# Splitting queries and keys of a head pair on 128 partitions at once, and spreading the parts by DMA

## The chip, the core and the metric

The kernel runs on one core of a Trainium2 chip. The metric is the device time of one execution in microseconds (us); several executions are made, and their median is compared.

## The reference

Two trunk layers of a latent diffusion block, on 512 latent tokens (a grid of 8 rows by 64 columns) and 256 context tokens of width 1024. Layer 0 mixes by differential attention, layer 1 by neighbourhood attention; each is followed by a squared-ReLU MLP, and both sublayers are normed, modulated and gated from a conditioning vector. What bears on the change:

```python
def rms_norm(x, g):
    xf = x.astype(jnp.float32)
    y = xf * lax.rsqrt(jnp.mean(xf * xf, axis=-1, keepdims=True) + NORM_EPS)
    return (y * g.astype(jnp.float32)).astype(x.dtype)

def diff_attend(q, k, v, lam):                      # layer 0: 8 heads, each a pair (m) of 64 columns
    s = jnp.einsum('bqhmd,bkhmd->bhmqk', q, k).astype(jnp.float32) * ATTN_SCALE
    p = jax.nn.softmax(s, axis=-1)
    w = (p[:, :, 0] - lam * p[:, :, 1]).astype(v.dtype)
    return jnp.einsum('bhqk,bkhe->bqhe', w, v)

    q_l = apply_axial_rope(proj_q(h_lat), cos, sin) # proj_q, proj_kv: h @ w, then rms_norm with a gain
    k_l, v_l = proj_kv(h_lat)
    k_l = apply_axial_rope(k_l, cos, sin)
    k_c, v_c = proj_kv(h_ctx)
    ...
    # layer 1: 16 heads of 64; q_row against a band of rows (with a bias) and all context keys
        s_loc = jnp.einsum('bqhd,brkhd->bhqrk', q_row, k_band).astype(jnp.float32) * ATTN_SCALE
        ...
        s_ctx = jnp.einsum('bqhd,bkhd->bhqk', q_row, k_c).astype(jnp.float32) * ATTN_SCALE
```

## The kernel before

Every float32 matrix operand is kept as two float32r parts, high and low (their sum is the value), and each product is made in three passes, high·high, high·low and low·high. A split of a block is therefore two operations: ScalarE (ACT) copies it with rounding into the high part, VectorE (DVE) or GpSimd (POOL) subtracts that from the source and writes the low part.

For scores of 64-column heads, both parts are stacked on the 128 partitions, so that one matmul contracts over high and low together. A query tile `q[:, m, :]` holds [high; low] for the pair's first head and [low; high] for its second; `kh[:, m, :]` holds the high part of the keys twice, `kl[:, m, :]` the low part twice. Scores are two matmuls, with `kh` and with `kl`.

The work runs in stages. In the profiled execution: setup and the first head's projections to about 90 us, attention of layer 0 to 440, output projection and norm to 560, the MLP to 1110, a transition to 1180, attention of layer 1 to 1500, its output projection to 1560, the second MLP to the end. In an attention stage two streams are interleaved by letters (`run`, with `ORD_HEAD` and `ORD_GROUP`): `attend0` or `attend1` of one head (layer 0) or group of two heads (layer 1), and the projections `qkv0` or `qkv1` of the next. Tokens go in six tiles of 128. `qkv0` steps through them with `tile_(i)` (projection matmuls at L346 into PSUM tile `A`, norm, values, and for the latent tokens the rotation on POOL) and `turn(t)` for pairs of tiles 0, 2 and 4: four transposes by TensorE into one PSUM bank, 256 columns of queries and 256 of keys with the pair's two heads on the lower and the upper 64 partitions, and then `q_split` and `k_split`. The first takes two ACT and two DVE operations of 64x256, the second four of each (the low parts' second copy is a DVE cast, L385). Layer 1 does the same, with queries for the latent tokens alone and with a gain. The turn of tiles 4 and 5 comes last in a head.

Weights come by `wload`: a DMA on SyncE's (SP's) queue into a raw tile `R` (two of them), ACT's copy (L99) and POOL's subtraction (L100) into a weight tile `W` (five of them). `load_qkv` loads the four slices a to d of a head; each holds two of the eight k-tiles, so that the eighth of a projection's k-tiles needs slice d. The modulation matrix is loaded into `R` tiles too (L113, four loads per head in layer 0), and layer 1 loads six bias rows per group on SP (L514). A framework of tiles inserts the waits; its scheduler fixes each engine's order when the program is built. Each queue runs strictly in that order.

Of the kernel before, what the change touches and what calls it, by code (L numbers as in the profile page):

```python
# [18 lines left out]
P = 128  # L19
# [15 lines left out]
# the order of the interleaved streams, by letters (see run)  # L35
# [5 lines left out]
# the PSUM tiles of each phase  # L41
# [8 lines left out]
class Block:  # L50
# [40 lines left out]
    def wload(self, src, n, tile=None, eng=None):  # L91
        """a weight slice [128, n] as its float32r parts: [:, 0] high, [:, 1] low."""
# [10 lines left out]
    def mod_load(self, l, n, early=False):  # L103
        """256 columns of the modulation matrix, as eight k-tiles."""
# [12 lines left out]
    def setup(self):  # L117
# [13 lines left out]
        # silu(c), silu(c_ctx), padded to 32 columns  # L131
# [8 lines left out]
        # modulation scalars: [layer][norm] -> A (gain*(1+scale)), B (shift)  # L140
# [28 lines left out]
        # lambda  # L169
# [66 lines left out]
    def normed(self, halves):  # L236
        """x rows (two halves of 512) -> x * rstd as one [128, 1024] tile."""
# [13 lines left out]
    def modulated(self, xns, tiles, l, norm, hT, tag):  # L251
        """transposes, modulates and splits the token tiles into hT."""
# [20 lines left out]
    def normed_early(self, xs):  # L273
        """the first norm, transposed, ahead of the modulation: 4 tiles of two k-tiles each."""
# [90 lines left out]
    def q_split(self, ps, q, cols, gain=None):  # L365
        """transposed queries of two heads -> stacked [H;L] (head 0), [L;H] (head 1)."""
        nc = self.nc
        lo, hi = slice(0, 64), slice(64, 128)
        for m, (a, b) in enumerate(((lo, hi), (hi, lo))):
            if gain is None:  # L370
                nc.scalar.activation(q[a, m, cols], ps[a], AF.Copy)
                nc.vector.tensor_sub(q[b, m, cols], ps[a], q[a, m, cols].bitcast(F32))
            else:
                nc.scalar.activation(q[a, m, cols], ps[a], AF.Copy, scale=gain[a])
                nc.vector.scalar_tensor_tensor(q[b, m, cols], ps[a], gain[a], q[a, m, cols].bitcast(F32),
                                               op0=ALU.mult, op1=ALU.subtract)

    def k_split(self, ps, kh, kl, cols):
        nc = self.nc
        lo, hi = slice(0, 64), slice(64, 128)  # L380
        for m, (a, b) in enumerate(((lo, hi), (hi, lo))):
            nc.scalar.activation(kh[a, m, cols], ps[a], AF.Copy)
            nc.vector.tensor_sub(kl[a, m, cols], ps[a], kh[a, m, cols].bitcast(F32))
            nc.scalar.activation(kh[b, m, cols], ps[a], AF.Copy)
            nc.vector.tensor_copy(kl[b, m, cols], kl[a, m, cols].bitcast(F32))  # L385

# [1 line left out]
    def load_qkv(self, w, g):  # L388
        return [self.wload(w[g, s], 768) for s in range(4)]

    def qkv0(self, w, hT, out, accs=None, tag='Q'):
# [26 lines left out]
        def turn(i):  # L418
# [7 lines left out]
            self.q_split(ps[:, 0:256], q, cols)  # L426
            self.k_split(ps[:, 256:512], kh, kl, cols)
# [10 lines left out]
    def attend0(self, h, qkv, last=None):  # L438
# [10 lines left out]
        for i in range(NT):  # L449
# [15 lines left out]
            # w = p0 - lam p1, up to the factor 1/sum0, which the output takes  # L465
# [40 lines left out]
    def bias1(self, g):  # L506
        """rpb of the windows (two heads, three kinds of tile) plus the window's mask, keys reversed."""
# [12 lines left out]
    def qkv1(self, w, hT, out, tag='H'):  # L520
# [16 lines left out]
        def turn(i0):  # L537
            ps = self.pst('A')
            for j in range(2):
# [20 lines left out]
    def attend1(self, g, qkv, last=None):  # L560
# [5 lines left out]
        for jp in range(2):  # L566
            for m in range(2):
# [19 lines left out]
                # the window that straddles tiles: [a 64 | b 128 | c 64] -> blocks b and [c | a]  # L587
# [110 lines left out]
    def mlp(self, l, t0, xh, hT, tag, mid, done, side):  # L698
# [36 lines left out]
        def blend():  # L735
            """x + gate * (the sum so far), beside the last matrix products."""
# [44 lines left out]
class Mods:  # L781
    """the modulation chunks, in order, each loaded well before its products."""
# [28 lines left out]
def hybrid_block(tc, a, out):  # L811
    nc = tc.nc
    with ExitStack() as ctx:
# [6 lines left out]
        with b.psum_phase("ps0", **PS_HEAD0):  # L820
# [4 lines left out]
            w = b.load_qkv(a["wqa"], 1)  # L825
            for _ in b.qkv0(None, hT, cur, accs):
                pass
        with b.psum_phase("psA", **PS_ATTN0):
            att = b.attend0(0, cur)
            run(mods, ORD_FIRST, a=att)  # L830
            for h in range(1, HEADS0):
                nxt = []
                qkv = b.qkv0(w if h == 1 else b.load_qkv(a["wqa"], h), hT, nxt)
# [29 lines left out]
        with b.psum_phase("psC", **PS_ATTN1):  # L863
            cur = []
            run(mods, "Q", q=b.qkv1(w1, hT1, cur))
            for g in range(GROUPS1):
                nxt, last = [], [] if g + 1 == GROUPS1 else None
                att = b.attend1(g, cur, last)
                if last is None:
                    w = b.load_qkv(a["wqb"], g + 1)  # L870
                    run(mods, ORD_GROUP, a=att, q=b.qkv1(w, hT1, nxt))
                else:
                    run(mods, ORD_OUT1, a=att, q=b.project(1, a["wob"], b.oT1, last, 2, lambda i: b.x2[i - 2], 'Q', 'H', 'S1', nxt))
# [16 lines left out]
def lay_out(i):  # L890
# [8 lines left out]
    # rotary tables, in the order of the permuted latents  # L899
# [55 lines left out]
```

## Time and profile before

| what | value |
|---|---|
| median of 3 runs | 1934.52 us (1934.1 to 1935.02) |
| span of the profiled execution | 1928.0 us |
| instructions | 27111 |
| busy: TensorE (PE) / DVE / ACT / POOL | 94% / 63% / 42% / 40% |
| DMA packets and bytes | 58723, 185.02 MB |

The span is that of the instructions of one execution under the profiler. The runs' times contain what lies around it: the median is 6.5 us longer. In rows of the profile, an instruction is given by engine, line, operation and `out<-in` with the names of the tiles (numbers left out); `SPq` and `ACTq` are the parts of an engine's queue that issue DMAs. PE counts matmuls, PEld the loading of weights into TensorE beside them.

### The profile page before, as it was taken

To read this page: it belongs to the slowest core of one execution; us is meant where nothing else is said; L and a number is where in the kernel's file an instruction comes from. 1 tells how busy PE (TensorE), PEld (TensorE's weight loads), DVE (VectorE), ACT (ScalarE), POOL (GpSimd) and SP (SyncE) were. 2 spreads that over 40 slices of the span, in tenths; PEclk is the share of its full clock that TensorE was granted. 3 is DMA by queue.
4 is the path that set the end of the run, shared out by engine and by line. 5 is a ranking of instruction groups with operands and counts; after the bars stand their busy time and mean duration, and the time that the engine had idled before them with its cause. 6 is when DMAs were issued, how large, how long until landed. Compare 5 with 4: busy or idle time off the path is not lost.

```text
span 1928.0 us, 27111 instructions
## 1 busy us (share of the span) xinstructions
PE 1809.4 (94%) x10256; PEld 1574.1 (82%) x10256; DVE 1205.3 (63%) x2349; ACT 812.5 (42%) x1819; POOL 770.6 (40%) x620
## 2 busy tenths in 40 slices
PE   6899999997899999999999988998998989999998
PEld 5788888885688888888888968998897778888886
DVE  4688888887664343343334685988889664444447
ACT  4466666666342221221221244666656342232231
POOL 3655555544222221221222443444543334344443
PEclk9999999998999999999999998999998999999999
DMA  7222222225222332332432241223323223323331
GB/s 296 92 67 71 86 85 74 73 69 195 84 89 90 118 120 91 128 124 95 131 113 74 57 125 41 50 62 74 77 72 99 93 77 100 97 87 94 103 94 71
DMA packets 58723, 185.02 MB, mean 96 GB/s; under 512 B 7328, under 2 KB 13792, under 8 KB 54496
## 3 DMA queue, kind: packets, MB, share of 16 engines
q1 hardware_dynamic: 52848, 173.44, 29.1%
q10 hardware_dynamic: 5744, 9.85, 1.4%
q8 instruction: 80, 1.31, 0.3%
q14 instruction: 51, 0.42, 0.1%
HBM read 174.45 MB, written 8.81 MB: 95 GB/s over the span
## 4 chain that ended last, share of the span: by engine, by line
PE 67%; DVE 15%; DMA 6%; ACT 4%; POOL 4%; issue 4%; SPq 1%; ACTq 0%; POOLq 0%; DVEq 0%
PE PD L719 23%; PE PA L753 11%; PE PB L753 10%; PE PA L346 9%; PE PA L651 4%; PE PA L200 2%; DMA X<-in_rpb_dram 2%; PE PS L458 2%; PE PB L485 1%; POOL W L100 1%; PE PQ L335 1%; DVE SA L581 1%; DMA N<-oT 1%; DMA R<-in_wmod_dram 1%; DVE N L604 1%
## 5 line engine op out<-in xcount | busy, mean ns | idle before, releaser
L100 POOL TENSOR_TENSOR W<-R,W 128x1024 fp32r<-128x1024 f32 (+1 forms) x200 | 451.0, 2262 | 700.8 <-ACT W L99 700.7
L99 ACT ACTIVATE W<-R 128x1024 fp32r<-128x1024 f32 (+1 forms) x204 | 200.9, 994 | 457.8 <-PE PB L753 364.2
L719 PE MATMUL PD<-Q,W 128*128 128x384 f32 (+1 forms) x1584 | 291.4, 332 | 1.1 <-DVE Q L270 0.5
L719 PEld LDWEIGHTS PD<-Q,W 128*128 128x128 f32 x1584 | 269.5, 188 | 16.6 <-issue 7.0
L346 PE MATMUL PA<-W,H 128*128 128x384 f32 x1008 | 201.8, 347 | 5.1 <-DVE T L209 4.4
L728 DVE TENSOR_TENSOR N<-N 128x768 f32<-128x768 f32 (+1 forms) x64 | 61.9, 969 | 220.3 <-ACT N L727 110.7
L346 PE MATMUL PA<-W,Q 128*128 128x384 f32 (+1 forms) x1008 | 186.7, 332 | 10.9 <-DVE H L535 5.6
L719 PE MATMUL PD<-H,W 128*128 128x512 f32 (+1 forms) x816 | 187.6, 386 | 3.4 <-DVE H L271 2.5
L346 PEld LDWEIGHTS PA<-W,H 128*128 128x128 f32 x1008 | 176.3, 191 | 13.0 <-DVE T L209 4.9
L719 PEld LDWEIGHTS PD<-H,W 128*128 128x128 f32 x816 | 148.9, 191 | 36.3 <-DVE H L271 2.7
L346 PEld LDWEIGHTS PA<-W,Q 128*128 128x128 f32 x1008 | 162.7, 198 | 13.3 <-DVE H L535 7.0
L753 PE MATMUL PA<-W,H 128*128 128x512 f32 x648 | 168.1, 399 | 2.7 <-DVE T L759 2.5
L233 POOL TENSOR_TENSOR SQ<-SQ,half 128x4 f32<-128x4 f32 (+1 forms) x96 | 93.9, 979 | 161.0 <-DVE SQ L231 133.9
L753 PEld LDWEIGHTS PA<-W,H 128*128 128x128 f32 x648 | 119.2, 188 | 32.9 <-issue 6.2
L753 PE MATMUL PB<-W,H 128*128 128x512 f32 x504 | 132.3, 394 | 0.0
L753 PE MATMUL PA<-W,Q 128*128 128x512 f32 x432 | 108.7, 391 | 2.2 <-ACT Q L730 1.7
L753 PEld LDWEIGHTS PB<-W,H 128*128 128x128 f32 x504 | 94.5, 188 | 19.4
L764 DVE TENSOR_TENSOR H<-PA,H 128x512 f32<-128x512 f32 x78 | 53.7, 688 | 78.6 <-PE PA L753 78.6
L753 PEld LDWEIGHTS PA<-W,Q 128*128 128x128 f32 x432 | 80.9, 188 | 21.1 <-ACT Q L730 2.4
L464 ACT ACTIVATE E<-PS,SA 128x768 f32<-128x768 f32 (+1 forms) x96 | 72.7, 758 | 34.4 <-DVE SA L463 33.8
L463 DVE TENSOR_REDUCE SA<-PS 128x1 f32<-128x768 f32 (+1 forms) x96 | 74.4, 775 | 20.2 <-ACT E L464 13.6
L753 PE MATMUL PB<-W,Q 128*128 128x512 f32 x336 | 85.3, 389 | 0.0
(213 smaller groups left out, 3177.1 us busy)
## 6 DMA issues: line engine op xcount, KB each, us to landing
R<-in_w_dram SPq DMA_DIRECT2D x128, 512.0 KB
W<-in_wmod_dram SPq DMA_DIRECT2D x32, 1024.0 KB
R<-in_wmod_dram SPq DMA_DIRECT2D x32, 512.0 KB
R<-in_wqa_dram SPq DMA_DIRECT2D x32, 384.0 KB
R<-in_wqb_dram SPq DMA_DIRECT2D x32, 384.0 KB
X<-in_rpb_dram SPq DMA_DIRECT2D x48, 128.0 KB
R<-in_woa_dram SPq DMA_DIRECT2D x8, 512.0 KB
R<-in_wob_dram SPq DMA_DIRECT2D x8, 512.0 KB
```

Source lines behind the costliest of these rows:

```text
L99: nc.scalar.activation(w[:, 0, :n], raw, AF.Copy)
L100: (eng or nc.gpsimd).tensor_sub(w[:, 1, :n], raw, w[:, 0, :n].bitcast(F32))
L200: nc.tensor.matmul(ps[32 * q:32 * q + 32, 0:256], self.silu[:, kt, :], raws[kt], start=kt < 4, stop=kt >= 4)
L233: nc.gpsimd.tensor_tensor(r, ss, self.half[:, :n], op=ALU.pow)
L346: nc.tensor.matmul(acc[:, :n], hT[kt][:, x, P * i:P * i + P], w[kt // 2][:, y, o:o + n], start=(kt == 0 and p == 0), stop=(kt == KT - 1 an ...
L463: nc.vector.tensor_reduce(mx, s, op=ALU.max, axis=AX, negate=True)
L464: nc.scalar.activation(e[:, m, :nk], s, AF.Exp, bias=mx[:, 0:1], accum_out=sm[:, m:m + 1])
L651: nc.tensor.matmul(ps, oHL[h][:, x, c:c + P], w[h // 2][:, y, 512 * (h % 2):512 * (h % 2) + 512], start=(h == hs[0] and p == 0), stop=(h = ...
L719: nc.tensor.matmul(ps[:, at:at + b1 - b0], w[kt // 4][:, x, o:o + P], hT[kt][:, y, b0:b1], start=(kt == 0 and p == 0), stop=(kt == KT - 1 ...
L728: nc.vector.tensor_mul(r, r, r)
L753: nc.tensor.matmul(ps, hd[:, x, P * i - c0:P * i - c0 + P], w[f][:, y, 512 * n:512 * n + 512], start=(f == 0 and p == 0), stop=(f == len(h ...
L764: nc.vector.tensor_add(av, ps, av)
```

## The change

`q_split` and `k_split` are replaced by three functions. `hl_split` splits the whole transposed block of a turn at once, one ACT and one DVE operation on 128 partitions (512 columns in layer 0; in layer 1 256 for the keys and, with the gain, 256 for the queries), into two scratch blocks `h` and `l`. `q_spread` and `k_spread` copy these to the stacked layout by DMAs of 64x256 on SP's queue: 4 for the queries, 8 for the keys. The scratch is the last 512 columns of the weight tiles themselves: `load_qkv` now allocates four tiles of 2048 columns, of which the weights use 1536. Turns 0 and 4 use the tails of the first two tiles, turn 2 those of the other two. The first group of layer 1, whose weights lie elsewhere, allocates four weight tiles for the purpose.

```diff
+    def hl_split(self, ps, h, l, gain=None):
+        nc = self.nc
+        if gain is None:
+            nc.scalar.activation(h, ps, AF.Copy)
+            nc.vector.tensor_sub(l, ps, h.bitcast(F32))
+        else:
+            nc.scalar.activation(h, ps, AF.Copy, scale=gain)
+            nc.vector.scalar_tensor_tensor(l, ps, gain, h.bitcast(F32), op0=ALU.mult, op1=ALU.subtract)
+
+    def q_spread(self, h, l, q, cols):
         nc = self.nc
         lo, hi = slice(0, 64), slice(64, 128)
         for m, (a, b) in enumerate(((lo, hi), (hi, lo))):
...
+            nc.sync.dma_start(q[a, m, cols].bitcast(F32), h[a].bitcast(F32))
+            nc.sync.dma_start(q[b, m, cols].bitcast(F32), l[a].bitcast(F32))
+
+    def k_spread(self, h, l, kh, kl, cols):
         nc = self.nc
         lo, hi = slice(0, 64), slice(64, 128)
...
+        for src, dst in ((h, kh), (l, kl)):
+            for m, a in enumerate((lo, hi)):
+                for b in (lo, hi):
+                    nc.sync.dma_start(dst[b, m, cols].bitcast(F32), src[a].bitcast(F32))
...
     def load_qkv(self, w, g):
-        return [self.wload(w[g, s], 768) for s in range(4)]
+        ts = [self.wpool.tile([P, 2048], F32R, tag="W", name=self._name("W")) for _ in range(4)]
+        return [self.wload(w[g, s], 768, t[:, 0:1536].rearrange("p (a n) -> p a n", a=2))
+                for s, t in enumerate(ts)], ts
+
+    def scratch(self, ts, k):
+        return [t[:, 1536:2048] for t in ts[2 * (k % 2):2 * (k % 2) + 2]]
...
-            self.q_split(ps[:, 0:256], q, cols)
-            self.k_split(ps[:, 256:512], kh, kl, cols)
+            h, l = self.scratch(room, i // 2)
+            self.hl_split(ps, h, l)
+            self.q_spread(h[:, 0:256], l[:, 0:256], q, cols)
+            self.k_spread(h[:, 256:512], l[:, 256:512], kh, kl, cols)
...
+            h, l = self.scratch(room, i0 // 2)
+            self.hl_split(ps[:, 0:256], h[:, 0:256], l[:, 0:256])
+            self.k_spread(h[:, 0:256], l[:, 0:256], kh, kl, slice(P * i0, P * i0 + 256))
             if i0:
-                self.q_split(ps[:, 256:512], q, slice(P * i0 - 256, P * i0), gain=self.gqk)
-            self.k_split(ps[:, :256], kh, kl, slice(P * i0, P * i0 + 256))
+                self.hl_split(ps[:, 256:512], h[:, 256:512], l[:, 256:512], gain=self.gqk[:, 0:1])
+                self.q_spread(h[:, 256:512], l[:, 256:512], q, slice(P * i0 - 256, P * i0))
...
+            room = [b.wpool.tile([P, 2048], F32R, tag="W", name=b._name("W")) for _ in range(4)]
+            run(mods, "Q", q=b.qkv1(w1, room, hT1, cur))
```

The order of the engines moves with it. The rows below are of heads 3 and 4 of layer 0 (each row is line, operation, `out<-in` with the tiles' numbers, shape; "x3" is three alike). On SP before, the loads of a head's four weight slices follow each other between loads of the modulation matrix (`R508`, `R509`, and `R642` behind):

```order
L113 DMA R508_2402<-in_wmod_dram 128x1024
L113 DMA R509_2403<-in_wmod_dram 128x1024
L95 DMA R625_2960<-in_wqa_dram 128x768
L95 DMA R627_2965<-in_wqa_dram 128x768
L95 DMA R629_2970<-in_wqa_dram 128x768
L95 DMA R631_2975<-in_wqa_dram 128x768
L113 DMA R642_3022<-in_wmod_dram 128x1024
```

On SP after, head 3's spreads stand between slice c (`R631`) and slice d (`R632`) of head 4's weights: first turn 0's, then turn 2's (out of `W475`, `W476`), then turn 4's (out of `W473`, `W474`); the rows from turn 2's keys on:

```order
L390 DMA Q482_2314<-W475_2295 64x256 x4
L390 DMA Q483_2315<-W476_2296 64x256 x4
L380 DMA Q481_2313<-W473_2293 64x256 x2
L381 DMA Q481_2313<-W474_2294 64x256 x2
L390 DMA Q482_2314<-W473_2293 64x256 x4
L390 DMA Q483_2315<-W474_2294 64x256 x4
L95 DMA R632_3000<-in_wqa_dram 128x768
```

What moved: slice d's load was behind slice c's, and now is behind 36 DMAs, of which the last 12 need the head's last split. On ACT before, three of the next head's slices (`W628`, `W630`, `W632`, L99) are split ahead of turn 2's queries (`PC585`, L371):

```order
L99 ACTIVATE W628_2967<-R627_2965 128x768
L99 ACTIVATE W630_2972<-R629_2970 128x768
L384 ACTIVATE Q482_2296<-PC541_2575 64x256
L354 ACTIVATE Y602_2861<-PA601_2836 128x256
L401 ACTIVATE Q484_2298<-PA601_2836 128x128
L99 ACTIVATE W632_2977<-R631_2975 128x768
L371 ACTIVATE Q481_2295<-PC585_2777 64x256
```

On ACT after, slice b (`W626`) comes behind turn 2's split (row L369 of `PC585`, ten rows earlier) and ahead of an exponential (L478) and of turn 4's split (`PC624`):

```order
L99 ACTIVATE W626_2985<-R630_2992 128x768
L478 ACTIVATE E607_2900,SA608_2901<-PS609_2902,SA610_2911 128x768
L369 ACTIVATE W473_2293<-PC624_2965 128x512
L502 ACTIVATE O596_2845<-PB595_2840,SA591_2829 128x128
L461 ACTIVATE N564_2715<-PB600_2855,subg_122 128x128
L99 ACTIVATE W627_2986<-R631_2996 128x768
```

What moved: slices b, c and d of the next head now come behind splits of this one, and slice b's tile is one out of which turn 2's spreads read. On PE after, between the last projection of head 3 and the first product of head 4 that needs slice d (`W628`) stand the scores of one query tile of head 2 and two of head 3, with their outputs; the rows at the end:

```order
L499 MATMUL PB617_2935<-Q330_1621,X614_2922 128x256 x12
L460 MATMUL PB622_2958<-ident_69,O555_2664 128x128
L472 MATMUL PS646_3052<-Q483_2315,Q481_2313 128x256
L472 MATMUL PS646_3052<-Q482_2314,Q481_2313 128x256
L472 MATMUL PS646_3052<-Q483_2315,Q481_2313 128x256
L472 MATMUL PS646_3052<-Q482_2314,Q481_2313 128x512
L472 MATMUL PS646_3052<-Q483_2315,Q481_2313 128x512
L460 MATMUL PB623_2961<-ident_69,O620_2952 128x128
L346 MATMUL PA637_3008<-W628_2987,H94_542 128x384
```

What stands there now: the product with slice d is in PE's queue behind the scores of head 3 that read the spread keys (`Q482`, `Q483`), and everything later stands behind it.

More of the change, by code (lines that the diff above doesn't have):

```diff
@@ L369, in q_split, with qkv0 @@
         for m, (a, b) in enumerate(((lo, hi), (hi, lo))):
[L370 to L378, printed above, removed]
+            nc.sync.dma_start(q[a, m, cols].bitcast(F32), h[a].bitcast(F32))
+            nc.sync.dma_start(q[b, m, cols].bitcast(F32), l[a].bitcast(F32))
+    def k_spread(self, h, l, kh, kl, cols):
         nc = self.nc
         lo, hi = slice(0, 64), slice(64, 128)
[L381 to L385, printed above, removed]
-    def load_qkv(self, w, g):
-        return [self.wload(w[g, s], 768) for s in range(4)]
-    def qkv0(self, w, hT, out, accs=None, tag='Q'):
+        for src, dst in ((h, kh), (l, kl)):
+            for m, a in enumerate((lo, hi)):
+                for b in (lo, hi):
+                    nc.sync.dma_start(dst[b, m, cols].bitcast(F32), src[a].bitcast(F32))
+    def load_qkv(self, w, g):
+        ts = [self.wpool.tile([P, 2048], F32R, tag="W", name=self._name("W")) for _ in range(4)]
[3 more added lines that the diff above has]
+        return [t[:, 1536:2048] for t in ts[2 * (k % 2):2 * (k % 2) + 2]]
+    def qkv0(self, w, room, hT, out, accs=None, tag='Q'):
         nc = self.nc
@@ L518, in bias1, with qkv1 @@
         return b
-    def qkv1(self, w, hT, out, tag='H'):
+    def qkv1(self, w, room, hT, out, tag='H'):
         nc = self.nc
@@ L824, in hybrid_block @@
             b.setup_layer0(*tabs)
-            w = b.load_qkv(a["wqa"], 1)
-            for _ in b.qkv0(None, hT, cur, accs):
+            w, room = b.load_qkv(a["wqa"], 1)
+            for _ in b.qkv0(None, room, hT, cur, accs):
                 pass
@@ L832, in hybrid_block @@
                 nxt = []
-                qkv = b.qkv0(w if h == 1 else b.load_qkv(a["wqa"], h), hT, nxt)
+                if h > 1:
+                    w, room = b.load_qkv(a["wqa"], h)
+                qkv = b.qkv0(w, room, hT, nxt)
                 att2 = b.attend0(h, nxt, last if h + 1 == HEADS0 else None)
@@ L869, in hybrid_block @@
                 if last is None:
-                    w = b.load_qkv(a["wqb"], g + 1)
-                    run(mods, ORD_GROUP, a=att, q=b.qkv1(w, hT1, nxt))
+                    w, room = b.load_qkv(a["wqb"], g + 1)
+                    run(mods, ORD_GROUP, a=att, q=b.qkv1(w, room, hT1, nxt))
                 else:
```

2 lines of the change are left out of this document (removed).

## The prediction

> **What bounds the kernel now.** I read the page from the top: the span, the busy time of each engine, then stretches of each attention layer, and last what TensorE (PE) waited for in them.
>
> ```profile
> span 1928.0 us, 27111 instructions
> PE 1809.4 (94%) x10256; PEld 1574.1 (82%) x10256; DVE 1205.3 (63%) x2349; ACT 812.5 (42%) x1819; POOL 770.6 (40%) x620
> 140.00:440.00 300.00, 280.17 (x1864) 252.30 (x1864) 244.70 (x585) 197.87 (x565) 159.37 (x195) 0.99 0.26 82
> 1180.00:1500.00 320.00, 293.49 (x1948) 280.84 (x1947) 274.78 (x650) 198.97 (x506) 138.95 (x143) 0.96 0.25 68
> ```
>
> The last two rows are a table of stretches (start:end, length, then busy PE, PEld, DVE, ACT, POOL, granted clock, DMA share, GB/s): six heads of layer 0, seven groups of layer 1. PE is busy 94% of the span. It idles 300 − 280.2 = 19.8 us in the first stretch (3.3 per head of 50 us) and 320 − 293.5 = 26.5 us in the second (3.8 per group). DVE comes next, at 82% and 86% of these stretches. The PE's waits, first in layer 0 and then in layer 1 (total us, times, longest):
>
> ```profile
> PE PA L200 <- DMA R<-in_wmod_dram: 5.3, 6, 1.5
> PE PB L485 <- DVE X L481: 4.6, 6, 1.8
> PE PC L424 <- ACT Q L384: 0.4, 1, 0.4
> PE PA L346 <- POOL W L100: 0.2, 1, 0.2
> ...
> PE PA L346 <- DVE H L535: 5.6, 4, 2.2
> PE PA L346 <- ACT H L384: 3.1, 1, 3.1
> PE PS L575 <- DVE H L375: 1.5, 1, 1.5
> PE PS L575 <- ACT H L384: 0.6, 1, 0.6
> ```
>
> The splits that the change rewrites make PE wait 0.4 us in six heads of layer 0, and 5.2 us in seven groups of layer 1. The projection (L346) hardly ever waits for its weights in layer 0: 0.2 us.
>
> **What it takes away.** The splits per turn, and the nearest rows for the wide ones that replace them:
>
> ```profile
> L384 ACT ACTIVATE Q<-PC 64x256 fp32r<-64x256 f32 x42 | 15.9, 378 | 9.0 <-DVE Q L383 8.4
> L372 DVE TENSOR_TENSOR Q<-PC,Q 64x256 fp32r<-64x256 f32 x42 | 17.7, 422 | 3.0 <-ACT Q L371 1.7
> L385 DVE CAST Q<-Q 64x256 fp32r<-64x256 f32 x48 | 24.1, 503 | 1.5
> L603 ACT ACTIVATE N<-PB x64: 577/598/605, 1213.0 to 1523.3; 128x512 fp32r<-128x512 f32 x64
> L604 DVE TENSOR_TENSOR N<-PB,N x64: 671/686/693, 1213.9 to 1524.0; 128x512 fp32r<-128x512 f32 x64
> ```
>
> A turn of layer 0 was 6 ACT x 0.38 = 2.3 us and 4 x 0.42 + 2 x 0.50 = 2.7 us on DVE; now it is one of each, 0.60 and 0.69 by the same shape at L603 and L604. That is 1.7 and 2.0 us a turn, over 24 turns 41 and 48 us; layer 1 gives about as much less, some 30 on each. None of it lies on PE's path but through PE's waits. Layer 0 can win between 0 and its 19.8 idle us; I take 1.3 per head, since the probabilities' splits (L481, 4.6) wait on a DVE that gets freer. In layer 1 I take the 5.2 us of the splits, the 5.6 behind L535 (it stands in DVE's queue, beside the splits) and 2 us of clock (below): 13 together, with bounds of 0 and 26.5.
>
> **What it adds: the spreads.** Each turn now issues 12 DMAs of 64x256 (64 KB) on SP's queue, the same queue that loads weights: 36 per head, 32 per group, 544 in all, of which before has none. Three rows bound SP's time for one:
>
> ```profile
> L210 ACTq DMA_DIRECT2D gates<-T x16: 229/237/257, 77.5 to 1036.4; - x16
> L95 SPq DMA_DIRECT2D R<-in_wqa_dram x32: 327/328/1651, 10.9 to 374.9; - x32
> L514 SPq DMA_DIRECT2D X<-in_rpb_dram x48: 537/591/667, 1138.5 to 1428.5; - x48
> 1225.69 1.25 SPq L514 DMA_DIRECT2D X<-in_rpb_dram  x2
> 1223.79 5.45 DMA X<-in_rpb_dram
> ```
>
> A plain block issued from SP is 0.33 us (L95), the nearest in form, so c = 0.33; ends 0.24 (a small transfer, on ACT's queue) and 0.59 (many short runs, L514). The last two rows, of the timeline and of the chain of waits, give the landing: the pair's issue ends at 1226.94, its bytes are there at 1229.24, 2.3 us later. The spreads of a turn thus take 12 x 0.33 + 2.3 = 6.3 us from the first issue to the last landing; ends 5.2 and 9.4. In the changed order each also waits for the one eight issues earlier, which at 2.3 us of landing asks for 0.33 too.
>
> By the Trainium skill (DMA: Bandwidth & Descriptors, Anatomy of one DMA) a transfer costs about 2 us plus its bytes at 436 GB/s, so a turn's 768 KB would be an estimated 3.8 us if the bytes and not the issues set it; the rows above say that issuing does, and no run here shows the other yet.
>
> **Where it meets PE in layer 0.** The parts wait in the last columns of the head's own four weight tiles, so a weight tile comes free for the next head only when the spreads that read it have landed. With five tiles, the next head's slice a is in the fifth, b and c take the tiles of turn 2's scratch, d takes one of turn 4's; d's load also stands on SP behind turn 4's spreads. Turn 0 and turn 4 share scratch too, but turn 0's spreads are a tile's projection older. So the end of a head becomes a chain, which the before kernel spreads under the projection. Its pieces:
>
> ```profile
> 219.00 0.33 SPq L95 DMA_DIRECT2D R<-in_wqa_dram  x1
> 222.14 0.84 ACT L99 ACTIVATE W<-R 128x768 fp32r<-128x768 f32 x1 [2.58 <-DMA R<-in_wqa_dram]
> 223.47 1.81 POOL L100 TENSOR_TENSOR W<-R,W 128x768 fp32r<-128x768 f32 x1
> 201.23 0.90 ACT L464 ACTIVATE E<-PS,SA 128x768 f32<-128x768 f32 x1
> 200.26 0.39 ACT L354 ACTIVATE Y<-PA 128x256 f32<-128x256 f32 x1 [1.61 <-PE PA L346]
> 211.77 0.73 POOL L416 TENSOR_TENSOR Y<-Y,Y 128x256 f32<-128x256 f32 x1
> ```
>
> A slice lands 222.14 − 219.33 = 2.8 us after its issue. With t = 0 at the end of the head's last projection matmul: turn 2's transposes lie 0.9 us before it; their split (0.60 + 0.69, two handovers) has both parts at 0.6. Twelve issues end at 4.6, the last lands at 6.9. Only then ACT splits slice b (0.84, to 7.7), an exponential follows (0.90, to 8.6), and turn 4's split stands behind both: done at 9.9. Turn 4's transposes must be there too: norm and rotation of the last tile took from 200.26 to 212.50 in before, its own pieces are about 5 us; I take 7.5, since nothing long stands ahead of it now; it hides under the 8.6, and at its 12.2 adds 3.6. Twelve issues to 13.9, slice d's issue and landing 0.33 + 2.8 to 17.0, its split on ACT and POOL 0.84 + 1.81 to 19.7.
>
> What PE has in the meantime, in the changed order, up to the first matmul that reads slice d: 19 projection matmuls (L346), 20 of scores (L458 in before), 20 of output (L485), 10 transposes of probabilities (L478) and 11 short ones:
>
> ```profile
> 202.06 4.28 PE L346 MATMUL PA<-W,H 128*128 128x384 f32 x23
> 206.18 0.49 PE L478 MATMUL PB<-ident,E 128*128 128x128 f32 x3
> 207.10 1.66 PE L458 MATMUL PS<-Q,Q 128*128 128x512 f32 x8
> 211.24 1.59 PE L485 MATMUL PB<-Q,X 128*128 128x256 f32 x12
> ```
>
> That is 19 x 0.186 = 3.5; 20 scores at up to 0.207, the narrow ones less, 3.5; 20 x 0.12 of output (they overlap a little) = 2.4; and 21 transposes and short ones at 0.09 to 0.16, some 2.0: 11.4 us, of which I count 11.3. So PE stands still for 19.7 − 11.3 = 8.4 us at each head's end. With c = 0.24 it is 6.2, with 0.59 14.9, with the slow transposes 12. Of the present 3.3 us per head 2 stay, after the 1.3 of relief: 8.4 + 2 − 3.3 = 7.1 us more per head. There are seven ends of a head; the one of head 0, whose projections run apart, I count half: 6.5 x 7.1 = 46 us. Ends: 6.5 x (6.2 − 3.3) = 19, where all present idling goes, and 6.5 x 14.9 = 97, where none does.
>
> **The clock.** After a wait PE is slower for a while:
>
> ```profile
> 1303.56 1.81 PE L346 MATMUL PA<-W,Q 128*128 128x256 f32 x13 [1.26 <-DVE H L535]
> 1311.89 4.85 PE L346 MATMUL PA<-W,Q 128*128 128x256 f32 x21 [3.09 <-ACT H L384]
> ```
>
> The same matmul took 0.139 us after a gap of 1.26 and 0.231 after 3.09: some 2 us lost in the 21. The 8.4 us are cut into pieces by exponentials and transposes, of which I expect one over 3 us in about every fourth head: 3 us; ends 0 and 6.5 x 2 = 13. The Trainium skill (TensorE: Matmul & The Clock Gate, Why this matters for your kernels) wants no idle gap above about 3 us; the two rows agree with it, and by it a single gap of 8.4 us would cost each head the 2 us, 13 in place of my 3.
>
> **Layer 1.** There three slices of a later group and its six bias rows stand on SP ahead of a group's spreads and one behind, the group has 32 spreads in place of 36, and its period of 45 us leaves SP idle for most of it. 32 x 0.33 = 10.6 us of issue fit. I take 0.5 us per group of new waits, 4 us, and 3 us more for the first group, whose scratch takes four weight tiles of its own, while its spreads stand behind twelve bias rows. With the 13 of relief that is −6; ends +15 and −25.
>
> **The sum.** 46 + 3 (clock) − 6 (layer 1) = 43 us on the span of 1928.0: 1971. The runs' median is 1934.5, 6.5 above the span, and I keep that distance: 1934.5 + 43, some 1977.
>
> **The rivals.** First, *the spreads are cheap and hide, and the engines' relief wins*: a 64 KB issue takes 0.1 us. Then turn 2's spreads are landed at 0.6 + 1.2 + 2.3 = 4.1, slice b's split and the exponential end at 5.8, the transposes are there (their own pieces, 5 us), turn 4's split ends at 7.1, its issues at 8.3, slice d is in at 11.4 and split at 14.1: PE waits 2.8 us per head, and if one more stays of the 3.3, layer 0 loses 6.5 x 0.5 = 3. Layer 1 gives its 13 and up to half as much again: 1934.5 + 3 − 17 = 1920. The place is L346's wait for slice d; it decides for faster where that wait is under about 3 us a head. Against it: no issue on SP's queue in these rows is under 0.33, and PE's wait at 0.24 is already twice 3 us.
>
> Second, *both effects cancel*: c at 0.24 (+19 in layer 0) against a layer 1 at −20: 1934.
>
> Third, *a half-height transfer costs what the L514 rows cost*: c = 0.59, wait 14.9 us per head, and layer 1's 19 us of issue per group then push the bias rows (its chain already has 5.45 us of DMA X): 6.5 x (14.9 + 2 − 3.3) = 88, and some 1.5 us a group, 12: 2035. In its favour stands a rule of the Trainium skill (DMA: Bandwidth & Descriptors, Rules for kernel authors): two transfers on the two halves of the partitions share the same engines, so that one of 128 rows does better. What hangs on it is that 12 of half height would cost like 12 of full height; no run here shows that yet.
>
> **How the numbers follow.** About 0.2%, 4 us, is what a measurement of this kernel can tell from no change. Chances: the forecast, 1945 to 2010, 0.63; the first rival 0.18; the second 0.05; the third 0.14. The likeliest is 1977. The range takes in the second rival and most of the first and of the third: 1920 to 2032. Faster 0.18, same 0.05, slower 0.77.
>
> **What would show it.** In the profile after: ACT's and DVE's instructions fall by 208 each (5 a turn in layer 0, 3 or 4 in layer 1), their busy time by some 70 us each; SP shows 544 transfers of L380, L381 and L390 at 0.33 us. In the stretch of layer 0 PE's waits have a new first row, L346 waiting for POOL's or ACT's split of W, with some 50 us where 0.2 stood, and ACT's L99 waits for DMAs out of W. The head period grows from 50 to about 57. In layer 1 L346's waits for L384's successor vanish. I am wrong if L346 has no such wait (issues are cheap, or the transposes come early), or if PE loses as much in layer 1: then SP's queue has no room there either.

## The result, and the profile after

The changed kernel took 2008.03 us (median of 4 runs, 2004.88 to 2012.18), the kernel before 1934.31 us beside it: a ratio of 1.0383, 95% interval 1.0362 to 1.0404, 74 us slower. The two profiles are of single executions, and their spans differ by 82 us and not by 74, since the one before, 1928.0 us, is some 5 us shorter than is usual for that kernel (43 executions beside the runs below have spans of 1927.1 to 1943.8, the middle one 1932.7), and the one after is the longest of its four. The top of its page:

```profile
span 2010.4 us, 27956 instructions
PE 1843.5 (92%) x10256; PEld 1583.8 (79%) x10256; DVE 1102.3 (55%) x2141; ACT 735.0 (37%) x1611; POOL 765.9 (38%) x620
```

The freed engines are there: 208 instructions less on DVE and on ACT, 103 and 78 us of busy time. PE's 10256 matmuls are the same, but their records add up to 34 us more. To see where the span grew, both traces are cut where a stage's first instruction starts: first projection of layer 0 to the first MLP (L719 before, L736 after), that MLP, and first score of layer 1 to the second MLP. The table of stretches, before and then after (start:end, length, busy PE, PEld, DVE, ACT, POOL, clock, DMA share, GB/s):

```profile
66.70:561.00 494.30, 450.13 (x2753) 392.23 (x2754) 386.87 (x898) 300.24 (x836) 239.59 (x273) 0.97 0.27 84
561.00:1110.10 549.10, 548.02 (x3089) 478.04 (x3088) 238.45 (x323) 127.09 (x167) 157.25 (x70) 1.00 0.33 108
1192.10:1555.90 363.80, 333.16 (x2118) 311.10 (x2117) 302.65 (x689) 216.27 (x535) 150.80 (x147) 0.95 0.26 70
```

```profile
68.90:605.70 536.80, 470.48 (x2753) 397.53 (x2754) 337.02 (x778) 260.05 (x716) 238.54 (x273) 0.95 0.38 113
605.70:1154.80 549.10, 547.98 (x3089) 477.95 (x3088) 238.35 (x323) 126.89 (x167) 157.46 (x70) 1.00 0.34 108
1238.90:1637.60 398.70, 341.26 (x2102) 311.40 (x2103) 255.06 (x597) 181.89 (x449) 154.44 (x149) 0.95 0.42 108
```

Layer 0 is 42.5 us longer, 22 of it idle PE and 20 longer records of the same matmuls; layer 1 is 34.9 longer, 27 and 8 (with 16 matmuls fewer between its marks). The MLP is unchanged to 0.1 us.

The longer records have two parts that the traces show. First, the trace grants the clock either in full or at half: at half for 34.1 us of layer 0's stretch before and 51.2 after, and for 34.1 and 42.8 of layer 1's. Half of the difference, 8.5 and 4.4 us, is the most that this can cost. Second, a projection matmul alone has a record of 0.337 us, but 23 in a row take 4.28 us, 0.186 each; so each further break in a row of matmuls adds some 0.15 us to the busy time, without PE doing more (an estimate from these two numbers). PE stops 104 times in layer 0's stretch after and 59 before, 74 and 45 times in layer 1's: 7 and 4 us. The two parts together are 15 of the 20 us and the 8.

What one spread costs SP, by line (duration min/median/max in ns):

```profile
L390 SPq DMA_DIRECT2D Q<-W x192: 461/595/1932, 78.3 to 498.2; - x192
L390 SPq DMA_DIRECT2D H<-W x192: 461/595/2095, 1221.0 to 1562.6; - x192
L95 SPq DMA_DIRECT2D R<-in_wqa_dram x32: 327/328/1452, 11.2 to 438.3; - x32
```

595 ns for a spread, while a weight load of six times the bytes stays at 328. The end of a head, SP, ACT's weight splits and PE in the timeline:

```profile
239.73 1.10 SPq L380 DMA_DIRECT2D Q<-W  x2
240.93 1.18 SPq L381 DMA_DIRECT2D Q<-W  x2
242.16 6.24 SPq L390 DMA_DIRECT2D Q<-W  x8
248.50 1.17 SPq L380 DMA_DIRECT2D Q<-W  x2
249.77 1.18 SPq L381 DMA_DIRECT2D Q<-W  x2
251.00 5.07 SPq L390 DMA_DIRECT2D Q<-W  x8
256.16 0.53 SPq L95 DMA_DIRECT2D R<-in_wqa_dram  x1
...
246.27 0.84 ACT L99 ACTIVATE W<-R 128x768 fp32r<-128x768 f32 x1
250.29 0.84 ACT L99 ACTIVATE W<-R 128x768 fp32r<-128x768 f32 x1 [1.30 <-DMA Q<-W]
259.68 0.84 ACT L99 ACTIVATE W<-R 128x768 fp32r<-128x768 f32 x1 [1.02 <-DMA R<-in_wqa_dram]
...
240.32 0.68 PE L346 MATMUL PA<-W,H 128*128 128x384 f32 x3
260.06 0.30 PE L460 MATMUL PB<-ident,O 128*128 128x128 f32 x1 [1.69 <-DVE O L508]
260.58 0.44 PE L346 MATMUL PA<-W,H 128*128 128x384 f32 x1 [0.22 <-ACT W L99]
262.47 1.97 PE L346 MATMUL PA<-W,H 128*128 128x384 f32 x5 [0.57 <-POOL W L100]
```

From 239.73 to 256.07 SP does nothing but issue 24 spreads, 16.3 us in a row. (In five other heads of this layer they are two rows of 12, 7.5 to 8.2 us each, with 0.6 to 1.5 us between them.) Slice d's load (256.16) stands behind them, lands at 259.68, and PE's first product with it starts at 260.58, 19.6 us after the last projection of the old head (241.0); the next ones, which need POOL's part of slice d too, start at 262.47. PE is busy for 12.5 of the 19.6 us and stands still for 7.1. But this idle time isn't in one place. PE's waits from head to head in layer 0 (us in total, times, longest):

```profile
PE PA L346 <- POOL W L100: 8.3, 14, 1.0
PE PB L460 <- DVE O L508: 8.0, 6, 1.7
PE PS L472 <- ACT E L478: 7.0, 10, 2.8
PE PB L499 <- ACT X L494: 4.8, 10, 0.6
PE PA L346 <- ACT W L99: 4.8, 6, 1.1
PE PS L472 <- DMA Q<-W: 3.4, 7, 1.0
```

The weights' splits (L99, L100) make 13 us in six heads; most of the rest is PE at the short chains of attention, one after the other, where no projection stands between them in its queue. In layer 1 the same row of spreads stands at the end of a group:

```profile
1325.03 4.97 SPq L390 DMA_DIRECT2D H<-W  x8
...
1332.84 5.02 SPq L390 DMA_DIRECT2D H<-W  x8
...
1340.51 1.04 SPq L95 DMA_DIRECT2D R<-in_wqb_dram  x2
1346.60 1.73 ACT L99 ACTIVATE W<-R 128x768 fp32r<-128x768 f32 x2 [3.15 <-DMA R<-in_wqb_dram]
1347.49 1.11 PE L346 MATMUL PA<-W,Q 128*128 128x256 f32 x3 [2.48 <-ACT W L99]
```

24 issues in 15.4 us, to 1340.4; the next weights behind them; PE waits 2.48 us for these, where in layer 1 before L346 waited longest for splits of DVE and ACT (L535, L384). Its waits in seven groups:

```profile
PE PS L592 <- ACT E L599: 10.5, 9, 2.8
PE PB L619 <- DVE T L635: 10.0, 8, 1.6
PE PS L592 <- DMA H<-W: 9.6, 14, 2.1
PE PB L629 <- DVE N L621: 6.3, 10, 1.4
PE PA L346 <- ACT W L99: 5.7, 5, 2.5
PE PA L346 <- POOL W L100: 5.0, 5, 1.1
```

The waits of L346 for DVE's and ACT's H are gone; in their place scores wait for landings (DMA H<-W, 9.6) and for exponentials, and L346 for the weights' splits, 10.7 us.

### The profile page after: what moved, and what is told of

Its sections match the earlier page's. It is cut to its first block, busy times and chain, and to the rows that moved or that the text cites. A ratio compares the mean times of both kernels' runs of the same rounds, so it can differ in the third digit from the quotient of the medians.

```text
span 2010.4 us, 27956 instructions
## 1 busy us (share of the span) xinstructions
PE 1843.5 (92%) x10256; PEld 1583.8 (79%) x10256; DVE 1102.3 (55%) x2141; ACT 735.0 (37%) x1611; POOL 765.9 (38%) x620
## 2 busy tenths in 40 slices
DMA packets 102248, 220.76 MB, mean 110 GB/s; under 512 B 16032, under 2 KB 57312, under 8 KB 98016
## 5 line engine op out<-in xcount | busy, mean ns | idle before, releaser
L100 POOL TENSOR_TENSOR W<-R,W 128x1024 fp32r<-128x1024 f32 (+1 forms) x200 | 451.2, 2265 | 741.1 <-ACT W L99 721.6
L99 ACT ACTIVATE W<-R 128x1024 fp32r<-128x1024 f32 (+1 forms) x204 | 200.4, 993 | 457.7 <-PE PB L770 364.3
L736 PE MATMUL PD<-Q,W 128*128 128x384 f32 (+1 forms) x1584 | 291.3, 332 | 1.1 <-DVE Q L270 0.6
L736 PEld LDWEIGHTS PD<-Q,W 128*128 128x128 f32 x1584 | 269.4, 188 | 16.7 <-issue 7.0
L346 PE MATMUL PA<-W,H 128*128 128x384 f32 x1008 | 210.2, 352 | 16.0 <-POOL W L100 8.9
L346 PEld LDWEIGHTS PA<-W,H 128*128 128x128 f32 x1008 | 176.5, 192 | 31.1 <-POOL W L100 15.5
L346 PE MATMUL PA<-W,Q 128*128 128x384 f32 (+1 forms) x1008 | 186.5, 331 | 12.4 <-POOL W L100 6.0
L736 PE MATMUL PD<-H,W 128*128 128x512 f32 (+1 forms) x816 | 188.3, 387 | 3.3 <-DVE H L271 2.5
L736 PEld LDWEIGHTS PD<-H,W 128*128 128x128 f32 x816 | 149.6, 193 | 36.3 <-DVE H L271 2.7
L346 PEld LDWEIGHTS PA<-W,Q 128*128 128x128 f32 x1008 | 160.8, 195 | 17.6 <-POOL W L100 8.2
L472 PE MATMUL PS<-Q,Q 128*128 128x256 f32 (+1 forms) x320 | 78.5, 370 | 12.4 <-ACT E L478 7.9
L499 PE MATMUL PB<-Q,X 128*128 128x256 f32 x448 | 74.0, 301 | 16.6 <-DVE X L495 11.4
```

Source lines behind the costliest of these rows:

```text
L99: nc.scalar.activation(w[:, 0, :n], raw, AF.Copy)
L100: (eng or nc.gpsimd).tensor_sub(w[:, 1, :n], raw, w[:, 0, :n].bitcast(F32))
L346: nc.tensor.matmul(acc[:, :n], hT[kt][:, x, P * i:P * i + P], w[kt // 2][:, y, o:o + n], start=(kt == 0 and p == 0), stop=(kt == KT - 1 an ...
L472: nc.tensor.matmul(s[:, c0:c1], q[:, m, P * i:P * i + P], k[:, m, c0:c1], start=p == 0, stop=p == 1)
L499: nc.tensor.matmul(po[:, :256], wT[:, x, P * kt:P * kt + P], v[:, kt].rearrange("p a d -> p (a d)"), start=(x, kt) == jobs[0], stop=(x, kt ...
L736: nc.tensor.matmul(ps[:, at:at + b1 - b0], w[kt // 4][:, x, o:o + P], hT[kt][:, y, b0:b1], start=(kt == 0 and p == 0), stop=(kt == KT - 1 ...
```

## The experiments

The theories: (1) SP's time for each issue, some 0.6 us, in rows of 24, holds the next weights and the scores; (2) the scratch holds the weight tiles until the spreads have landed; (3) the added bytes disturb. Beside the times, each profile gives two marks: the start of the first MLP, which carries layer 0, and the time from there to the start of the second, which carries layer 1 (the MLP in it is constant). A mark is read from one execution. Where a layer is as before, it came out 2.7 us later (layer 0 in the kernel with layer 1 alone) and 0.5 us earlier (layer 1 in the kernel with layer 0 alone), so a few us between two marks tell nothing. The two differences of marks add up to 3 to 8 us more than the difference of the times.

| kernel | time, us | before beside it | ratio (95%) | first MLP starts | to the second |
|---|---|---|---|---|---|
| before | 1934.31 | | | 561.0 | 994.9 |
| the change | 2008.03 | 1934.31 | 1.0383 (1.0362 to 1.0404) | 605.7 | 1031.9 |
| layer 0 alone | 1971.82 | 1936.44 | 1.0179 (1.0163 to 1.0194) | 602.1 | 994.4 |
| layer 1 alone | 1970.65 | 1936.44 | 1.0170 (1.0155 to 1.0186) | 563.7 | 1031.2 |
| free spreads | 1915.76 | 1936.44 | 0.9894 (0.9877 to 0.9911) | 566.3 | 972.3 |
| high parts on ACT's queue | 2025.35 | 1936.44 | 1.0453 (1.0428 to 1.0477) | 613.8 | 1042.5 |
| weights on ACT's queue | 1976.19 | 1934.04 | 1.0219 (1.0193 to 1.0245) | 584.9 | 1019.5 |
| own scratch, layer 0 | 1991.97 | 1934.04 | 1.0299 (1.0272 to 1.0325) | 584.9 | 1031.3 |
| own scratch, layer 1 | 2027.47 | 1934.16 | 1.0475 (1.0450 to 1.0501) | 601.8 | 1050.1 |
| six spreads a turn | 1952.09 | 1934.04 | 1.0095 (1.0065 to 1.0125) | 566.0 | 1011.5 |
| six, and weights on ACT | 1947.68 | 1934.16 | 1.0064 (1.0038 to 1.0090) | 568.6 | 1006.0 |
| three spreads a turn | 1944.93 | 1935.33 | 1.0050 (1.0032 to 1.0067) | 562.3 | 1009.0 |
| two for the keys' copies | 1931.78 | 1934.04 | 0.9988 (0.9974 to 1.0002) | 567.9 | 992.5 |
| keys' copies on POOL | 1947.29 | 1934.16 | 1.0061 (1.0041 to 1.0080) | 570.2 | 1002.9 |

**One layer at a time.** The other layer keeps its old splits and its own load of weights:

```diff
-            self.hl_split(ps, h, l)
-            self.q_spread(h[:, 0:256], l[:, 0:256], q, cols)
-            self.k_spread(h[:, 256:512], l[:, 256:512], kh, kl, cols)
+            self.q_split(ps[:, 0:256], q, cols)
+            self.k_split(ps[:, 256:512], kh, kl, cols)
```

(for layer 1 alone; the like for layer 0 alone.) Expected:

> The change in layer 0 alone; layer 1 keeps the 64x256 splits and its own weight tiles. By the marks in the trace (start of the first MLP 561.0 before, 605.7 after) layer 0 carries 45 of the 74 us: 1934 + 43 = about 1977. If the two layers' losses depended on each other (a clock or a DMA load that lasts), it would be off that by more than 8 us.

> The change in layer 1 alone. The prediction's step gives layer 1 a net gain of 6 us: 1928. The trace's marks (first score of layer 1 to start of the second MLP, 363.8 us before, 398.7 after) give a loss of 35: 1968.

35.4 and 34.2 us: they add up to 69.6 of the 74, so each layer carries its own half, and layer 1's forecast gain is refuted.

**Free spreads.** The split stays, its parts go nowhere, and queries and keys are filled with other data:

```diff
-            self.q_spread(...)
-            self.k_spread(...)
+        for n, t in enumerate((q, kh, kl)):
+            nc.sync.dma_start(t.bitcast(F32), hT[n].bitcast(F32))
```

> Wide splits as in the change, but their parts go nowhere: queries and keys are filled by three DMAs a head or group of the same total bytes, which wait for no split and read no weight tile (the scores are of other data). Theory 1 (SP's 0.6 us an issue, in a row, hold weights and scores) and theory 2 (weight tiles come free only on landing) both say that the loss is gone and the freed ACT and DVE show: 1915 to 1930. Theory 3 (the bytes themselves, by contention, slow PE and the weights) says that most of it stays: 1980 to 2005.

20.7 us faster than before, with as many bytes moved (220.65 MB, 220.76 in the change): theory 3 falls. All of the gain is in layer 1 (972.3 against 994.9); layer 0 is no faster (566.3). That is a ceiling: the scores here wait for no query or key at all, so it holds more than the engines' relief. The granted clock of layer 1's stretch is higher in it too, 0.99 against 0.95.

**Half of the issues on ACT's queue.**

```diff
-            nc.sync.dma_start(q[a, m, cols].bitcast(F32), h[a].bitcast(F32))
+            nc.scalar.dma_start(q[a, m, cols].bitcast(F32), h[a].bitcast(F32))
```

(and the high parts of the keys.)

> The high parts' spreads are issued from ACT's queue, the low parts' from SP's: 6 and 6 a turn. Theory 1: the 24 issues in a row at a head's end become 12 on SP, 7 us less per head or group, of which ACT's own 12 issues (0.35 to 0.6 us each, ahead of exponentials) take some back: 1945 to 1970. Theory 2: landing is hardly earlier by more than a few us: 1990 to 2005.

Slower by 15 us more than the change, which neither theory had. The profile of this kernel shows what stands behind it: an issue costs ACT the same,

```profile
L390 ACTq DMA_DIRECT2D Q<-W x96: 468/607/2011, 74.3 to 506.3; - x96
L390 SPq DMA_DIRECT2D Q<-W x96: 461/596/1718, 78.0 to 506.3; - x96
```

and the exponential stands behind the issues, as its timeline has it:

```profile
256.99 0.61 ACTq L390 DMA_DIRECT2D Q<-W  x1
257.67 0.59 ACTq L390 DMA_DIRECT2D Q<-W  x1
259.11 0.48 ACTq L390 DMA_DIRECT2D Q<-W  x1
259.63 0.61 ACTq L390 DMA_DIRECT2D Q<-W  x1
260.29 0.47 ACT L478 ACTIVATE E<-PS,SA 128x256 f32<-128x256 f32 x1 [0.79 <-issue]
```

In six heads of layer 0 PE then waits 12.9 us for ACT's weight splits, 4.8 in the change. The queue's price goes with the spread to the queue that issues it.

**Weights on ACT's queue.** `load_qkv`'s slices are loaded with `nc.scalar.dma_start` instead of `nc.sync.dma_start`.

> The heads' and groups' weight slices are loaded from ACT's queue, so that slice d's load no longer stands behind the spreads on SP; the scratch stays in the weight tiles. Theory 1 (SP's row of issues): slice d is in up to 3.5 us earlier per head and group, 14 of them, less what ACT's issues cost it: 1965 to 1990. Theory 2 (the tile comes free only when the spreads out of it have landed, whatever the load does): 2000 to 2010.

32 us come back, 21 in layer 0 and 12 in layer 1: having the next slices behind the spreads was that much of the loss, ACT's own issues already taken off.

**Scratch in tiles of its own.**

```diff
-            h, l = self.scratch(room, i // 2)
+            hl = self.sbt('N', [P, 1024], F32R)
+            h, l = hl[:, 0:512], hl[:, 512:1024]
```

> In layer 0 the scratch lies in tiles of its own (1024 columns of the N tiles), so that no weight tile waits for a spread; the spreads stay on SP; layer 1 is as in the change. Theory 2: layer 0's 35 us go: 1970 to 1975, as the change in layer 1 alone. Theory 1: SP still issues 36 spreads a head among the weight loads: 1990 to 2008.

> In layer 1 the scratch lies in N tiles, so that no weight tile waits for a spread; layer 0 and the queues are as in the change. Theory 2 for layer 1 (the tile's hold): 10 us or more of its 37 come back, 1985 to 2000, as 16 of 35 did for the same edit in layer 0. Theory 1: 2003 to 2012; the N tiles are shared with the probabilities, which may cost a few us.

In layer 0 16 us come back (21 by the mark). But the order moved with it: turn 4's spreads now stand behind the next head's first three slices on SP, so it doesn't tell the tile's hold from the queue. In layer 1 it lost 19 us more, probably since the N tiles there are the probabilities' (PE's longest sums of waits in that kernel are on DVE's T and N, 18.5 and 15.2 us). As a test of theory 2 both are inconclusive.

**Fewer issues, the same bytes.** Six spreads of full height, and then three, which land unstacked:

```diff
-            nc.sync.dma_start(q[a, m, cols].bitcast(F32), h[a].bitcast(F32))
-            nc.sync.dma_start(q[b, m, cols].bitcast(F32), l[a].bitcast(F32))
+            nc.sync.dma_start(q[:, m, cols].bitcast(F32), t.bitcast(F32))      # six: t is h or l
+        self.nc.sync.dma_start(q[:, :, cols].bitcast(F32),
+                               l[:, None, :].to_broadcast([P, 2, 256]).bitcast(F32))   # three
```

> Six spreads of 128x256 a turn in place of twelve of 64x256, the same bytes and the same waits, but the parts land unstacked (the scores are of other data). If SP's price is one per issue, 0.6 us, the row of issues at a head's end falls from 16 to 8 us, and most of the loss goes: 1925 to 1950. If it goes by rows or bytes, an issue takes 1.2 us and nothing changes: 2000 to 2010.

> Three spreads a turn (two in a context turn of layer 1), each of 128x2x256 (256 KB), in place of twelve of 64 KB: the same bytes, the same waits for the split, the same hold on the weight tiles, a quarter of the issues (the parts land unstacked, so the scores are of other data). Issues of 0.6 us are then under 2 us a turn. If the number of issues is what is left of the loss in the version with six (1952), the time comes near the free spreads: 1916 to 1928. If what is left is the 2 us of landing ahead of scores and weight tiles, it stays: 1940 to 1952.

SP's price for the keys' spreads in the kernel with six, and then in the one with three, by line:

```profile
L386 SPq DMA_DIRECT2D Q<-W x96: 465/599/1838, 73.6 to 462.9; - x96
```

```profile
L382 SPq DMA_DIRECT2D Q<-W x48: 593/608/1402, 76.0 to 447.6; - x48
```

0.6 us for 64 KB, for 128 and for 256, and 592 ns for the 768 KB of a free spread: among these copies from SBUF to SBUF (the on-chip memory that holds the tiles) the price is one per issue. The DMA packets are nearly as many as in the change (98 and 96 thousand against 102), so it isn't their number that costs. By their times the two kernels give back 56 and 64 of the 74 us. With 36, 18 and 9 issues a head, layer 0 ends 44.7, 5.0 and 1.3 us later than before. The scratch still lies in the weight tiles and the bytes are the same, so in layer 0 neither the hold nor the bytes is a loss by itself. With fewer issues the scheduler also puts slice d's load ahead of turn 4's spreads, so the price and the place in the queue go together here. In layer 1 it is 37.0, 16.6 and 14.1 us later: the number explains 23 of the 37, and the step from six to three brings almost nothing. So the run with six came out 2 us above the range for a price per issue, and the run with three within the range for a loss that stays. What is left in layer 1, PE's and then ACT's waits in the version with three:

```profile
PE PS L583 <- ACT E L590: 22.2, 16, 2.8
...
PE PS L583 <- DMA H<-W: 2.3, 7, 0.7
...
ACT W L99 <- DMA H<-W: 14.6, 14, 1.4
```

ACT's weight splits stand still for landings of spreads 14 times, which is theory 2's wait, and scores wait for exponentials, which are on that queue too. That the one causes the other is not shown: the exponentials themselves wait longest for DVE (L589, 47.1 us).

> Both remedies of theory 1 together: six spreads of 128x256 a turn (unstacked parts, so the scores are of other data) and the weight slices' loads on ACT's queue. If SP's row of issues was the whole loss, this comes near the free spreads (1916): 1920 to 1935. Each alone gave back 56 and 32 us of 74; if they remove the same wait, the sum stays at 1945 to 1952, and what is left is the weight tiles' hold or the landing ahead of the scores.

The two remedies together (1947.68) are 4 us below the six alone, and the two intervals overlap (1.0038 to 1.0090, 1.0065 to 1.0125): they take away the same wait, the second of the two expectations. What is left in layer 1 with three spreads is 14 us against before by the marks (the whole kernel is 9.6 slower by its times), and 37 against the free spreads. It lies in what three spreads have and free spreads don't: scores and weight tiles that wait for a split's way through the DMA (landing, tile's hold, and the order that the scheduler makes of them). Which of these it is was not separated.

**Parts of the idea in the kernel before.** The keys' second copies alone by DMA, two a turn, out of the keys' own tiles (a tile per head with high and low beside each other):

```diff
-            nc.scalar.activation(kh[b, m, cols], ps[a], AF.Copy)
-            nc.vector.tensor_copy(kl[b, m, cols], kl[a, m, cols].bitcast(F32))
+            nc.sync.dma_start(k[b, :, cols].bitcast(F32), k[a, :, cols].bitcast(F32))
```

> The kernel before with one thing of the change: the second copy of the keys' parts comes by DMA, two of 64x512 a turn (high and low of a head beside each other), in place of two ACT and two DVE operations; no scratch in weight tiles. About half of the relief that the free spreads showed (20 us), against 4 issues, some 2.5 us of SP, at a head's end: theory 1 says 1922 to 1932. If the landing of the copies before the scores is what costs (2 us a turn), it is 1936 to 1950.

No difference that can be told (0.9988, interval to 1.0002). Nor do the marks tell one by layer: the profiled execution is the longest of its ten. And the low copies on POOL:

```diff
-            nc.vector.tensor_copy(kl[b, m, cols], kl[a, m, cols].bitcast(F32))
+            nc.gpsimd.tensor_copy(kl[b, m, cols], kl[a, m, cols].bitcast(F32))
```

> The kernel before with the keys' second low parts (L385) copied by POOL in place of DVE; no DMA at all. DVE loses two of 0.38 to 0.50 us a turn; POOL gets two of about 0.4. If layer 1's 22 us of relief (free spreads) come from DVE's share, a quarter to a third of it: 1926 to 1931. If POOL, which makes the weights' low parts, delays them: 1934 to 1940.

13 us slower, beyond both expectations. POOL's copy takes 394 ns, where the middle one of DVE's took 290 (their mean, 503, is drawn up by some of up to 1911):

```profile
L385 POOL CAST Q<-Q x48: 391/394/1009, 75.9 to 470.2; 64x256 fp32r<-64x256 f32 x48
```

In layer 1 POOL also stands still for 41.8 us, in 23 waits for DVE's subtraction (L383) ahead of the copy, with its other work behind; whether that is the loss was not tried. Of the versions whose scores are of the right data none beat the kernel before by more than its interval.

## Why the prediction was right, and where it was not

Right in direction, and inside its range; the middle, +43 us, was little more than half of +74. That 2008 still lies in the forecast's own 1945 to 2010 is in part luck: the price of a spread was the third rival's and not the forecast's, layer 0 lost less than forecast, and layer 1, which was to gain, lost as much as layer 0. By its steps:

- *The splits.* 0.60 and 0.69 us a wide one were taken; L369 took 598 ns, L370 687. The instruction counts fell by the 208 forecast. DVE gave 50 us in layer 0 (48 forecast) but 48 in layer 1 (30 forecast).
- *SP's time for a spread*, 0.33 us, was wrong: 0.595, the upper end that had been kept for the range. It was taken from L95 as nearest in form, a load out of DRAM. The number of rows, 64 or 128, and the kilobytes don't matter to it, as the kernels with fewer issues show; nor does the length of a row, which is 1 KB in a spread and 6 KB in a free one (595 and 592 ns). Nor is it the wait for the transfer eight issues earlier that the prediction names: eight issues take 5.1 us, and a spread's bytes are there 1.9 us after its issue (the last of turn 2's ends at 248.40, and ACT's L99, which waits for it, starts at 250.29). A turn's twelve issues took 7.5 to 8.8 us, against the 3.8 given beside the landing for the bytes: the issues set it. This is the third rival's price. What the rival hung on the rule of the Trainium skill (DMA: Bandwidth & Descriptors, Rules for kernel authors: use one transfer of 128 partitions in place of two on the halves, which share the same engines) holds by the run with six, where 128 rows cost SP what 64 did, 599 against 595 ns. That price is SP's time; whether the halves share the DMA engines no run here shows.
- *The chain at a head's end* was 19.7 us to the end of slice d's split on POOL; in the head shown, the products that need POOL's part start after 21.5 us, and the one that needs ACT's alone after 19.6. PE stood still for 7.1 of these, against 8.4. Two errors nearly cancelled: the issues were slower, but SP stood in one row from 239.73 to 256.07, because slice b's tile needs only eight of the twelve landings, and its split and the exponential lay beside the issues and not between them.
- *Where the idle time shows* was wrong: the profile was to have L346's wait for weights at some 50 us. It has 13 in six heads. The rest is at L460, L472 and L499. The period of a head grew from 50.8 to 56.9 us (six periods between the first and the last of seven stores of the heads' outputs, 168.9 to 473.8 and 162.9 to 504.0), as the "50 to about 57" said.
- *The clock* was put at 3 us for layer 0; half of the added time at half clock is 8.5. *Layer 0* in all: 46 + 3 forecast, 44.7 by the mark, but 35.4 when it was changed alone. In its parts the 46 us of idle PE were 22, and the rest were the longer matmul records, most of which had no term. The sum came near, the parts were not right.
- *Layer 1*, −6 us, is the step that failed most: +37.0 by the marks, 34.2 with layer 1 alone. It said that 32 issues fit into a period of 45 us. They do, as a share; but 24 of them stand in one row at the group's end, 15.4 us, with the next weights behind and the scores waiting for the last to land. The price alone doesn't make up for it: with nine issues in place of 36 a head, and 8 in place of 32 a group, layer 1 still ends 14 us late by the mark. The reasoning that was used for layer 0, what stands behind the row, wasn't applied there. The relief in layer 1, 13 us, is not refuted by the 22.6 of the free spreads, which is a ceiling; it was outweighed.
- *The rivals.* The first (hidden spreads, the relief wins) gave 1920; the kernel in which they are free came to 1916, near it, and its condition, an issue of 0.1 us, is not met. The third had the right price and 2035: 88 us for layer 0 and 12 for layer 1, where 35 and 34 came of each alone. In layer 0 it let the price act without overlap, and in layer 1 it looked at the bias rows and not at what stands behind the row of spreads.
- *The distance of 6.5 us* compared the time of one execution with the span of another: in the 199 executions that have both, the time is 1.7 to 3.4 us above the span. It was kept on both sides, so the forecast difference doesn't hang on it.

## What to carry to other kernels

A DMA has a price on the queue that issues it, 0.6 us here for a copy within SBUF whether it carried 64 KB or 768, and it is paid by what stands next in that queue: count issues, not bytes, and look at the longest row of them and what is behind it, not at the queue's share over a period. Moving such issues to another engine's queue moves the price with them. Before trading an engine's work for DMAs, ask whether PE waits for that engine at all: in layer 0 it waited 0.4 us, and even free spreads gained nothing there.

## What was not expected of the hardware

SP's time for one DMA did not depend on its size between 64 KB and 768 KB or on 64 against 128 partitions (595, 599, 608, 592 ns), but was 328 ns for weight loads of 384 KB out of DRAM and 335 ns on ACT for a head's output of 384 KB into DRAM. All copies from SBUF to SBUF in these kernels took 0.47 to 0.62 us (medians by line). That both ends lie in SBUF isn't the whole of it, since the bias rows out of DRAM (L514) take 591 ns too; what makes the difference was not tried. ACT takes the same 0.6 us for a spread (607 ns). And the loss was not all idle time: of the changed kernel's 82 us of longer span, 34 are longer records of the same 10256 matmuls. Between 162.9 and 504.0 us after, half clock was granted seven times though PE never stood still for more than 2.8 us at once; in the six heads before it was three times.
